# Splitting the weights of two mixers and the first FFN panels one layer ahead, into a pair of parts in DRAM

## The chip, the cores and the metric

The kernel runs on one core of one Trainium2 chip. It is one program that goes once through eight layers. The metric is the device time of one execution in microseconds (us); what counts is the median of several executions. The profile and the trace belong to one further execution, recorded by the hardware profiler.

## The reference

One sequence of 512 tokens with 1024 channels, in float32, passes through four layers of a first block (mixers a, b, c, a) and four of a second (a mixer and an FFN, twice). The change touches the weights of the second block:

```python
def sandwich(x, g_pre, g_post, fn):
    return x + rmsnorm(fn(rmsnorm(x, g_pre)), g_post)

def swiglu(h, w_gate, w_up, w_down):
    return (jax.nn.silu(h @ w_gate) * (h @ w_up)) @ w_down

def even_mixer(t, layer_idx, w_in, lq1, lk1, lq2, lk2, subln, dw_w, dw_b, ln_g, ln_b, w_out, cos, sin):
    proj = t @ w_in
    y_a = diff_attention(proj[..., :3 * DIFF_WIDTH], layer_idx, lq1, lk1, lq2, lk2, subln, cos, sin)
    y_b = conformer_conv(proj[..., 3 * DIFF_WIDTH:], dw_w, dw_b, ln_g, ln_b)
    return jnp.concatenate([y_a, y_b], axis=-1) @ w_out

def odd_mixer(...):
    proj = t @ w_in
    ...
    y_c = s5_ssm(proj[..., :o1], a_re, a_im, ...)
    y_d = mla_attention(proj[..., o1:o2], proj[..., o2:o3], proj[..., o3:], ...)
    return jnp.concatenate([y_c, y_d], axis=-1) @ w_out
```

`diff_attention` takes the softmax of two score maps per head and subtracts one from the other; `conformer_conv` is a causal depthwise convolution of width 31 over 512 channels with a layer norm; `s5_ssm` is a linear recurrence over time; `mla_attention` is attention with compressed keys and values. Each weight matrix is used once per execution.

## The kernel before

**Stages.** The layers run in the order a0, b, c, a1, m0 (the even mixer), f0 (its FFN), m1 (the odd mixer), f1. In the trace c lies at about 950 to 1255 us, a1 to 1642, m0 to 1950, f0 to 2330, m1 to 2575 and f1 to the end. Activations are held transposed, as eight tiles of 128 channels x 512 tokens.

**Products in three parts.** A float32 product is made on TensorE (PE) from three products of fp32r operands (`mm3`, L287): each factor is split into a high part h, the value rounded to fp32r, and a low part l, the rest; then h·h, h·l and l·h are summed in PSUM. So each weight chunk, usually 128 x 1024 float32 or 512 KB, goes through three steps in `wchunk` (L273): SyncE (SP) issues its load into a tile `wr` (`fetch`, L252 to L255), ScalarE (ACT) copies it rounded into `wh` (L280), and VectorE (DVE) writes `wl` = `wr` - `wh` (L284; in the profile the line is L205, that of the wrapper that records every PE and DVE operation). The pool `pw` holds three buffers each of `wr`, `wh` and `wl`, so a chunk can be fetched and split while PE still works on the ones ahead.

**Who splits.** GpSimd (POOL) takes over the subtraction in two places: in m0, from `project(0)` on, for every third chunk (`share`, L271 to L276), and in `sandwich_end` for the chunks W1 and W2 (L975, L989). It does so in two pieces of 512 columns, whose rows carry the line L284.

**Panels.** `gemm_T` (L328) makes one output panel of 128 channels: a chunk, 24 matmuls of 512 tokens, and then a `tick()`. `gemm_tok` (L363) makes a token-major product from four chunks of the same size, with a tick after each. A tick advances every generator in the list `tasks` by one step (L296); `drain()` (L301) runs them to their end. Attention heads, the convolution and the tables of the recurrence are such tasks. The tasks settle the program order. Outside pinned stretches a scheduler then sets a fixed order for each engine, and every engine works through its own order one instruction after another, each with its waits. So an instruction that waits holds up all that stands behind it on that engine.

**m0.** Eight panels (`m0_wab`) yield the convolution's input. The convolution (`conv`, L1074) then runs as a task: per tile of 128 channels, 23 taps on DVE, as one multiply and 22 multiply-adds into the tile `cv`, and 8 taps on ACT and POOL into `cvg` (L1092). Meanwhile PE makes the projections for heads 0 and 1 (`project(0)`), the values, and `project(1)`. DVE also turns the query and key tiles by their rotary angles (the tiles `t`) and takes the maximum of each row of scores (`Ps`, `mxc`), which the exponential of the softmax needs. The scores lie in PSUM tiles called `a`; the panels' sums in those called `g`.

**m1.** The panels of `m1_win` come first, then keys, values and queries (`m1_wk`, `m1_wv`, `m1_wq`), while the recurrence runs as a task, with its scans and products on DVE (tiles `t`) and tables `E` and `bc` loaded from DRAM. They were stored there by `ssm_tables`, a task in f0 (L1595).

**Ends.** Each mixer of the second block and each FFN ends in `sandwich_end` (L891): the last output panels, the norm, the update of the eight tiles of x, and the first four panels of the layer that follows (W0 to W3 from `srcs`), which are thus split ahead, inside the end of the layer before. PE's and DVE's orders are fixed by hand there.

**c.** `layer_c` (L828) has two halves; each runs, twice, four panels of `c_wx`, four of `c_wz` and four half-size ones of `c_wg`, and then eight of `c_wo`.

Of the kernel before, what the change touches and what calls it, by code (L numbers as in the profile page):

```python
# [4 lines left out]
P = 128  # L5
# [174 lines left out]
def build(nc, tc, A, out, stages=("a0", "b", "c", "a1", "m0", "f0", "m1", "f1")):  # L180
# [40 lines left out]
    with ctx:  # L221
# [48 lines left out]

        share = [0, 0]  # L271

        def wchunk(src, n, eng=None):  # L273
            if eng is None:
                share[1] += 1
                eng = G if share[0] and share[1] % share[0] == 0 else V  # L276
            wr = early.pop(0) if early else fetch(src, n)
            wh = tl(pw, (P, 1024), "wh", F32R)
            wl = tl(pw, (P, 1024), "wl", F32R)
            S.activation(wh[:, :n], wr[:, :n], AF.Copy)  # L280
            step = n if eng is V else 512
            for o in range(0, n, step):
                e = slice(o, o + step)
                eng.tensor_tensor(wl[:, e], wr[:, e], f32(wh[:, e]), op=SUB)  # L284
            return wh, wl
# [542 lines left out]
        def layer_c(nxt):  # L828
            with ExitStack() as c:
# [7 lines left out]
                for t in pads:  # L837
                    V.memset(t[:, 0:16], 0.0)
                npad = [0]

# [4 lines left out]
                for half in range(2):  # L845
                    Y = []
                    for g in (2 * half, 2 * half + 1):
                        wd = 2 << g
                        M = []
                        for i in range(4):  # L850
                            ps = first.pop(0) if first else gemm_T(A["c_wx"][g * 4 + i], X)
                            xc = pad()
                            V.tensor_tensor(xc[:, 16:], ps, sb, op=MUL)
                            a, sh = xc, 1
                            while sh < wd:
                                b = pad() if sh * 2 < wd else tl(pp, (P, 16 + NT), "last", bufs=2)
                                (G if sh > 1 else V).tensor_tensor(
                                    b[:, 16:], a[:, 16:], a[:, 16 - sh:16 + NT - sh], op=ADD)
                                a, sh = b, sh * 2
                            df = tmp()  # L860
                            V.scalar_tensor_tensor(df, a[:, 16:], 1.0 / wd, xc[:, 16:], op0=MUL, op1=SUB)
                            fx = tl(psm, (P, 16), "fx")
                            V.tensor_tensor(fx, a[:, 16:32], ic[:, g * 16:g * 16 + 16], op=MUL)
                            V.tensor_tensor(df[:, :16], fx, xc[:, 16:32], op=SUB)
                            M.append(split(pp5, "m", df))
                        Z = []
                        for i in range(4):
                            pz = gemm_T(A["c_wz"][g * 4 + i], X)
                            z = tl(pp, (P, NT), "z", bufs=5)
                            V.tensor_tensor(z, pz, sb, op=MUL)  # L870
                            S.activation(z, z, AF.Silu)
                            Z.append(z)
                        for i in range(4):
                            ps = gemm_T(A["c_wg"][g, i], M)
                            V.scalar_tensor_tensor(Z[i], ps, csc[:, g * 4 + i:g * 4 + i + 1], Z[i],
                                                   op0=MUL, op1=MUL)
                            Y.append(split(py, "y", Z[i]))
                    for m in range(KD):
                        ps = gemm_T(A["c_wo"][half, m], Y)
                        V.tensor_tensor(xs[m], xs[m], ps, op=ADD)  # L880
                        if half:
                            finish_x(m)()

        def ffn_first(l):
            return [A[f"f{l}_w{n}"][i] for i in range(2) for n in "gu"] if f"f{l}" in stages else None

        def m1_first():
            return [A["m1_win"][i] for i in (2, 0, 1, 3)] if "m1" in stages else None


        def sandwich_end(W, Y, O, fresh, grow, srcs, pre=None, k0=0):  # L891
# [82 lines left out]
            if srcs:  # L974
                W1 = wchunk(srcs[1], D, G)  # L975
            begin(c, two)
# [3 lines left out]
            if srcs is None:  # L980
# [7 lines left out]
                return  # L988
            W2 = wchunk(srcs[2], D, G)  # L989
            X = state["X"]  # L990
# [54 lines left out]
        def layer_m0(nxt):  # L1045
            with ExitStack() as c:
                pm = newpool(c, "pm")
                pa = newpool(c, "pm0a", 8)
                X = state["X"]
                first, sc, sb = opening([A["m0_wab"][i] for i in range(3)], X)  # L1050
                new_norm(nxt)
# [75 lines left out]
                for i in range(4):  # L1127
                    pu = first.pop(0) if first else gemm_T(A["m0_wab"][2 * i], X)
                    pb = first.pop(0) if first else gemm_T(A["m0_wab"][2 * i + 1], X)
                    b = tmp()  # L1130
# [13 lines left out]
                def project(a):  # L1144

                    pss = gemm_tok([A["m0_wqk"][a, i] for i in range(4)], X, NT, 2)
                    q = tl(pm, (P, 4, 8, 64), "qk")
# [26 lines left out]
                def attend(h, T):  # L1174
# [53 lines left out]
                tasks.append(attend(3, T[1]))  # L1228
                share[0] = 0
                while any(Y[k] is None for k in range(4)):  # L1230
                    tick()
                sandwich_end(A["m0_wo"], Y, [tl(pa, (P, NT), "qkT") for _ in range(KD)], True, 8, ffn_first(0), k0=4)


# [132 lines left out]
        def layer_m1(nxt):  # L1367
            with ExitStack() as c:
# [91 lines left out]
                def glu():  # L1460
# [3 lines left out]
                    yield  # L1464
                    wh, wl = wchunk(A["s_wg"], 512)
                    for m in range(2):
# [26 lines left out]
                for i in range(2):  # L1493
                    ps = gemm_T(A["m1_win"][4 + i], X)
                    ss.add(ps, i)
                    CQ.append(split(py, "y", ps, qg[:, i:i + 1]))
# [4 lines left out]

                wh, wl = wchunk(A["m1_wk"], 768)
                KN = []
                for h in range(6):
# [6 lines left out]
                    if h % 2:  # L1511
                        tick()
                wh, wl = wchunk(A["m1_wv"], 768)
                vt = tl(pm, (P, 4, 768), "vt")
# [10 lines left out]
                for a in range(3):  # L1525
                    wh, wl = wchunk(A["m1_wq"][a], 1024)
                    for b in range(4):
# [51 lines left out]
                O = [t[:, a] for t in [tl(pm, (P, 2, NT), "E", bufs=3) for _ in range(3)] for a in range(2)]  # L1579
                sandwich_end(A["m1_wo"], Y, O + [tl(pm, (P, NT), f"u{i}") for i in range(2)], True, 10, ffn_first(1))  # L1580


        def layer_f(l, nxt):
            with ExitStack() as c:
# [30 lines left out]

        pdr0 = newpool(ctx, "pdr0", space=bass.MemoryType.DRAM)
        mag = tl(pc, (P, 8), "mag")
# [41 lines left out]
```

## Time and profile before

| what | value |
| --- | --- |
| median of 3 executions | 2931.03 us |
| lowest, highest | 2930.87, 2932.01 us |
| the profiled execution, its own time | 2936.18 us |
| span of the profiled execution | 2933.7 us |
| mean granted TensorE clock over the span | 0.976 of full speed |
| PE busy | 2820.6 us, 96% |
| DVE busy | 1642.2 us, 56% |
| ACT busy | 1051.9 us, 36% |
| POOL busy | 347.3 us, 12% |
| moved by DMA | 270.08 MB, 92 GB/s over the span |

The profiled execution's own time is that of the device; the span is what the profiler saw from its first to its last instruction, and 2.5 us lie around it. Busy time counts an engine's instructions and not its waits. PE is the engine that is busy nearly all the time; its clock can be lowered by the chip, and the granted clock says by how much in a stretch.

### The profile page before, as it was taken

Reading aid. Unit: us, or ns where it says so; the run is one execution under the profiler, and the core shown is the slowest. Engines: PE = TensorE matmul, PEld = TensorE weight load, DVE = VectorE, ACT = ScalarE, POOL = GpSimd, SP = SyncE. Lnnn points to the kernel's source line nnn. Section 1 sums busy time; section 2 is a strip of 40 time slices with the busy share of each in tenths; the row PEclk is TensorE's granted clock in tenths of the full one; section 3 lists DMA queues with packets and bytes.
Section 4 is the critical chain, followed back from the end, with each engine's and each line's share of the span. In section 5 each row is a group of like instructions: output and inputs, shape, how many; then the busy total and the mean of one; then the engine's idle time right before and its main releaser. Section 6 shows DMA issues by size and latency. Waiting matters only on the chain. (4 is left out here: it accounts for less than half of the span.)

```text
span 2933.7 us, 34524 instructions
## 1 busy us (share of the span) xinstructions
PE 2820.6 (96%) x13488; PEld 2331.9 (79%) x13488; DVE 1642.2 (56%) x3023; ACT 1051.9 (36%) x1679; POOL 347.3 (12%) x272
## 2 busy tenths in 40 slices
PE   8999999999999999999999987889999979999998
PEld 7888888888888888888888865678888845888886
DVE  4454654545556554544445697896443696543434
ACT  4322344444444322333223445442222435432222
POOL 2000000000000111210010252120000341300001
PEclk9999999999999999999999997889999999999999
DMA  4222332222223232322222211123332320132222
GB/s 161 94 86 94 129 111 87 87 80 94 72 94 95 94 101 89 120 93 94 93 94 92 90 63 44 48 96 136 111 105 92 113 90 22 58 101 100 94 99 67
DMA packets 87667, 270.08 MB, mean 92 GB/s; under 512 B 11728, under 2 KB 18640, under 8 KB 87504
## 3 DMA queue, kind: packets, MB, share of 16 engines
q1 hardware_dynamic: 87504, 267.88, 27.6%
q8 instruction: 105, 1.72, 0.2%
q14 instruction: 58, 0.48, 0.1%
HBM read 255.26 MB, written 12.58 MB: 91 GB/s over the span
## 5 line engine op out<-in xcount | busy, mean ns | idle before, releaser
L280 ACT ACTIVATE wh<-wr 128x1024 fp32r<-128x1024 f32 (+2 forms) x464 | 479.9, 1035 | 1329.8 <-PE g L205 1015.7
L205 DVE TENSOR_TENSOR wl<-wr,wh 128x1024 fp32r<-128x1024 f32 (+2 forms) x454 | 566.3, 1248 | 341.3 <-ACT wh L280 338.7
L205 PE MATMUL g<-xl,wh 128*128 128x512 f32 (+1 forms) x1720 | 661.6, 385 | 17.2 <-DVE xl L205 17.0
L205 PE MATMUL g<-xh,wh 128*128 128x512 f32 (+1 forms) x1720 | 663.7, 386 | 0.7 <-ACT wh L280 0.7
L205 PE MATMUL g<-xh,wl 128*128 128x512 f32 (+1 forms) x1720 | 658.1, 383 | 0.8 <-DVE wl L205 0.8
L205 PE MATMUL g<-wh,xh 128*128 128x512 f32 (+1 forms) x992 | 383.1, 386 | 16.9 <-ACT wh L280 8.9
L205 PE MATMUL g<-yh,wh 128*128 128x512 f32 (+1 forms) x1046 | 394.9, 378 | 1.4 <-DVE qr L205 1.4
L205 PE MATMUL g<-yh,wl 128*128 128x512 f32 (+1 forms) x1046 | 391.4, 374 | 3.1 <-DVE wl L205 3.1
L205 PEld LDWEIGHTS g<-xl,wh 128*128 128x128 f32 x1720 | 327.1, 190 | 83.0 <-DVE xl L205 22.9
L205 PE MATMUL g<-yl,wh 128*128 128x512 f32 (+1 forms) x1046 | 391.2, 374 | 0.0
L205 PE MATMUL g<-wl,xh 128*128 128x512 f32 (+1 forms) x992 | 377.8, 381 | 0.5 <-DVE wl L205 0.5
L205 PEld LDWEIGHTS g<-xh,wl 128*128 128x128 f32 x1720 | 327.3, 190 | 63.2 <-DVE wl L205 1.4
L205 PE MATMUL g<-wh,xl 128*128 128x512 f32 (+1 forms) x992 | 376.6, 380 | 0.0
L205 PEld LDWEIGHTS g<-xh,wh 128*128 128x128 f32 x1720 | 327.5, 190 | 61.2 <-ACT wh L280 1.2
L424 POOL TENSOR_TENSOR acc<-acc,t 128x256 f32<-128x256 f32 (+1 forms) x111 | 129.8, 1170 | 1654.5 <-issue 1406.4
L205 PEld LDWEIGHTS g<-wh,xh 128*128 128x128 f32 x992 | 188.5, 190 | 50.4 <-ACT wh L280 8.9
L205 PEld LDWEIGHTS g<-yh,wh 128*128 128x128 f32 x1046 | 198.4, 190 | 37.9 <-DVE qr L205 1.8
L205 PEld LDWEIGHTS g<-yh,wl 128*128 128x128 f32 x1046 | 198.1, 189 | 38.1 <-DVE wl L205 4.2
L205 PEld LDWEIGHTS g<-yl,wh 128*128 128x128 f32 x1046 | 198.3, 190 | 35.4 <-issue 1.2
L205 DVE TENSOR_TENSOR t<-g,sb 128x512 f32<-128x512 f32 x112 | 77.2, 690 | 251.4 <-PE g L205 251.4
L205 PEld LDWEIGHTS g<-wh,xl 128*128 128x128 f32 x992 | 188.4, 190 | 34.7 <-issue 0.2
L205 PEld LDWEIGHTS g<-wl,xh 128*128 128x128 f32 x992 | 188.6, 190 | 33.9 <-DVE wl L205 1.6
(315 smaller groups left out, 2728.5 us busy)
## 6 DMA issues: line engine op xcount, KB each, us to landing
wr<-in_f_wg_dram SPq DMA_DIRECT2D x44, 512.0 KB, 3.5
wr<-in_f_wu_dram SPq DMA_DIRECT2D x44, 512.0 KB, 3.5
wr<-in_a_wv_dram SPq DMA_DIRECT2D x32, 512.0 KB, 3.5
wr<-in_a_wu_dram SPq DMA_DIRECT2D x32, 512.0 KB, 3.4
wr<-in_a_wz_dram SPq DMA_DIRECT2D x32, 512.0 KB, 3.4
wr<-in_a_wo_dram SPq DMA_DIRECT2D x32, 512.0 KB, 3.5
wr<-in_b_wc_dram SPq DMA_DIRECT2D x32, 512.0 KB, 3.5
wr<-in_f_wd_dram SPq DMA_DIRECT2D x32, 512.0 KB, 3.5
```

The source lines that it names most:

```text
L205: r = f(*a, **k)
L280: S.activation(wh[:, :n], wr[:, :n], AF.Copy)
L424: G.tensor_tensor(self.acc[:, t], self.acc[:, t], sq[:, t], op=ADD)
```

## The change

A class `Pre` names a chunk together with two DRAM tiles for its parts, h and l. A task `presplit` makes them: per step SP loads a chunk into the tile `pr`, ACT writes `ph`, DVE writes `pl`, and SP stores both parts to DRAM. `pr` has one buffer, `ph` and `pl` have two each. A step ends right after its load was issued, and its split comes with the next tick. `wchunk` of a `Pre` then loads the parts straight into `wh` and `wl` by two DMAs and splits nothing. The sharing with POOL is gone, for these chunks and for W1 and W2.

The task runs twice: in c, for the 28 chunks of m0 and the first four panels of f0; and in f0 from its third pair of panels on, beside `ssm_tables`, for the 20 chunks of m1 and the first four panels of f1. Layer c drains it before its last eight panels.

```diff
-
-        def wchunk(src, n, eng=None):
-            if eng is None:
-                share[1] += 1
-                eng = G if share[0] and share[1] % share[0] == 0 else V
-            wr = early.pop(0) if early else fetch(src, n)
+        pdr0 = newpool(ctx, "pdr0", space=bass.MemoryType.DRAM)
+
+        class Pre:
+
+
+            def __init__(self, src, n):
+                uid[0] += 1
+                self.src, self.n = src, n
+                self.h, self.l = (tl(pdr0, (P, n), f"pre{a}{uid[0]}") for a in "hl")
+
+        def presplit(pool, todo):
+            made = []
+
+            def store():
+                w, wh, wl = made.pop(0)
+                nc.sync.dma_start(w.h, f32(wh))
+                nc.sync.dma_start(w.l, f32(wl))
+            for w in todo:
+                n = w.n
+                wr = tl(pool, (P, 1024), "pr")[:, :n]
+                wh, wl = (tl(pool, (P, 1024), "p" + a, F32R, bufs=2)[:, :n] for a in "hl")
+                nc.sync.dma_start(wr, w.src)
+                if made:
+                    store()
+                yield
+                S.activation(wh, wr, AF.Copy)
+                V.tensor_tensor(wl, wr, f32(wh), op=SUB)
+                made.append((w, wh, wl))
+            store()
+
+        def wchunk(src, n):
             wh = tl(pw, (P, 1024), "wh", F32R)
             wl = tl(pw, (P, 1024), "wl", F32R)
+            if isinstance(src, Pre):
+                nc.sync.dma_start(f32(wh[:, :n]), src.h)
+                nc.sync.dma_start(f32(wl[:, :n]), src.l)
+                return wh, wl
+            wr = early.pop(0) if early else fetch(src, n)
             S.activation(wh[:, :n], wr[:, :n], AF.Copy)
-            step = n if eng is V else 512
-            for o in range(0, n, step):
-                e = slice(o, o + step)
-                eng.tensor_tensor(wl[:, e], wr[:, e], f32(wh[:, e]), op=SUB)
+            V.tensor_tensor(wl[:, :n], wr[:, :n], f32(wh[:, :n]), op=SUB)
             return wh, wl
 
         def mm3(ps, ah, al, bh, bl, start, stop):
...
                     V.memset(t[:, 0:16], 0.0)
+                if "m0" in stages:
+                    tasks.append(presplit(newpool(c, "pre"), m0_weights() + (ffn_first(0) or [])))
                 npad = [0]
 
...
                             V.scalar_tensor_tensor(Z[i], ps, csc[:, g * 4 + i:g * 4 + i + 1], Z[i],
                                                    op0=MUL, op1=MUL)
                             Y.append(split(py, "y", Z[i]))
+                    if half:
+                        drain()
                     for m in range(KD):
                         ps = gemm_T(A["c_wo"][half, m], Y)
                         V.tensor_tensor(xs[m], xs[m], ps, op=ADD)
                         if half:
                             finish_x(m)()
 
+        PRE = {}
+
+        def pre(name, *ix):
+            k = (name,) + ix
+            if k not in PRE:
+                a = A[name]
+                for i in ix:
+                    a = a[i]
+                PRE[k] = Pre(a, a.shape[-1])
+            return PRE[k]
+
         def ffn_first(l):
-            return [A[f"f{l}_w{n}"][i] for i in range(2) for n in "gu"] if f"f{l}" in stages else None
+            return [pre(f"f{l}_w{n}", i) for i in range(2) for n in "gu"] if f"f{l}" in stages else None
 
         def m1_first():
-            return [A["m1_win"][i] for i in (2, 0, 1, 3)] if "m1" in stages else None
+            return [pre("m1_win", i) for i in (2, 0, 1, 3)] if "m1" in stages else None
+
+        def m0_weights():
+            return ([pre("m0_wab", i) for i in range(8)] + [pre("m0_wqk", a, i) for a in range(2) for i in range(4)]
+                    + [pre("m0_wv", i) for i in range(4)] + [pre("m0_wo", m) for m in range(KD)])
+
+        def m1_weights():
+            return (m1_first() + [pre("m1_win", i) for i in (4, 5)] + [pre("m1_wk"), pre("m1_wv")]
+                    + [pre("m1_wq", a) for a in range(3)] + [pre("s_wg")] + [pre("m1_wo", m) for m in range(KD)])
 
 
         def sandwich_end(W, Y, O, fresh, grow, srcs, pre=None, k0=0):
...
             if srcs:
-                W1 = wchunk(srcs[1], D, G)
+                W1 = wchunk(srcs[1], D)
...
-            W2 = wchunk(srcs[2], D, G)
+            W2 = wchunk(srcs[2], D)
...
-                share[:] = [3, 0]
                 q = project(0)
                 T = [flip_qk(q, 0), flip_qk(q, 1)]
-                pss = gemm_tok([A["m0_wv"][i] for i in range(4)], X, NT, 2)
...
                         if l == 0 and i == 2 and "m1" in stages:
+                            tasks.append(presplit(newpool(c, "pre"), m1_weights() + (ffn_first(1) or [])))
                             tasks.append(ssm_tables(ptab))
                         pg = first.pop(0) if first else gemm_T(A[f"f{l}_wg"][i], X)
                         pu = first.pop(0) if first else gemm_T(A[f"f{l}_wu"][i], X)
```

The other uses of m0's and m1's weights are changed in the same way, from `A["m0_wo"][m]` to `pre("m0_wo", m)` and so on. `pdr0` moves from the end of `build` to this place.

In the orders below, an operation's output stands before the arrow and its inputs behind it.

DVE in m0, before, at the first row maximum of the attention. `cv` are taps of the convolution, `wl` low parts of weights, `ISA Ps` the maximum.

```order
L205 TENSOR_TENSOR wl_13345<-wr_13342,wh_13344 128x1024
L205 SCALAR_TENSOR_TENSOR cv_2314_12738<-up_2313_12735,m_dw_12571,cv_2314_12738 128x512
L205 SCALAR_TENSOR_TENSOR cv_2327_12822<-up_2326_12819,m_dw_12571,cv_2327_12822 128x512
L205 SCALAR_TENSOR_TENSOR cv_2314_12738<-up_2313_12735,m_dw_12571,cv_2314_12738 128x512
L205 SCALAR_TENSOR_TENSOR cv_2327_12822<-up_2326_12819,m_dw_12571,cv_2327_12822 128x512
L205 ISA Ps_13266,mxc_13267<-a_13264,cmask_12592 128x128
L205 ISA mxc_13267 128x1
L205 ISA Ps_13272,mxc_13273<-a_13270,cmask_12592 128x128
L205 ISA mxc_13273 128x1
```

DVE at the same place, after.

```order
L205 SCALAR_TENSOR_TENSOR cv_2500_13050<-up_2499_13047,m_dw_12889,cv_2500_13050 128x512
L205 SCALAR_TENSOR_TENSOR cv_2511_13130<-up_2510_13127,m_dw_12889,cv_2511_13130 128x512
L205 TENSOR_TENSOR cv_2500_13050<-cv_2500_13050,cvg_13424 128x512
L205 SCALAR_TENSOR_TENSOR cv_2511_13130<-up_2510_13127,m_dw_12889,cv_2511_13130 128x512 x14
L205 ISA Ps_13553,mxc_13554<-a_13551,cmask_12910 128x128
L205 ISA mxc_13554 128x1
L205 ISA Ps_13559,mxc_13560<-a_13557,cmask_12910 128x128
L205 ISA mxc_13560 128x1
L205 RECIPROCAL d_2576_13550<-d_2576_13550 128x2
```

The first maximum now stands behind all 88 multiply-adds of the convolution, where 78 stood ahead of it before, and no `wl` lies among them.

SP in c, before, at the half's output panels: one fetch per panel.

```order
L254 DMA wr_8571<-in_c_wg_dram 128x512
L254 DMA wr_8595<-in_c_wo_dram 128x1024
L254 DMA wr_8627<-in_c_wo_dram 128x1024
L254 DMA wr_8659<-in_c_wo_dram 128x1024
L254 DMA wr_8691<-in_c_wo_dram 128x1024
```

SP at the same panels, after: `pr` is the load of the chunk that is split ahead, `preh` and `prel` are the stores of its parts.

```order
L254 DMA wr_8908<-in_c_wo_dram 128x1024
L286 DMA preh_1497_7917<-ph_8784 128x1024
L292 DMA pr_8815<-in_m_wo_dram 128x1024
L287 DMA prel_1498_7918<-pl_8785 128x1024
L254 DMA wr_8948<-in_c_wo_dram 128x1024
L286 DMA preh_1500_7919<-ph_8816 128x1024
L292 DMA pr_8859<-in_m_wo_dram 128x1024
L287 DMA prel_1501_7920<-pl_8817 128x1024
L254 DMA wr_8988<-in_c_wo_dram 128x1024
```

Each fetch of a panel now stands behind the load of `pr` and both stores; the load of `pr` itself cannot start before DVE has written the `pl` before it, since there is one buffer.

ACT at these panels, after.

```order
L296 ACTIVATE ph_8816<-pr_8815 128x1024
L309 ACTIVATE wh_8946<-wr_8948 128x1024
L296 ACTIVATE ph_8860<-pr_8859 128x1024
L309 ACTIVATE wh_8986<-wr_8988 128x1024
L296 ACTIVATE ph_8900<-pr_8899 128x1024
L309 ACTIVATE wh_9026<-wr_9028 128x1024
```

A `ph` now stands ahead of each `wh`, one for one; before, `wh` alone stood for the weights here. The task's last 13 chunks go in this way, one beside each full panel; counted back further, its last 20 go beside 19 full panels and four half ones.

## Rows read from the trace of the kernel before

**Rows 1.** The page's part 1: busy us (share of the span), number of instructions.

```profile
PE 2820.6 (96%) x13488; PEld 2331.9 (79%) x13488; DVE 1642.2 (56%) x3023; ACT 1051.9 (36%) x1679; POOL 347.3 (12%) x272
```

**Rows 2.** Windows (c, m0, m1): length; PE, PEld, DVE, ACT, POOL; clock; DMA; GB/s.

```profile
1100.00:1150.00 50.00, 50.00 (x223) 41.39 (x222) 21.82 (x32) 10.83 (x12) 8.99 (x6) 1.00 0.27 89
...
1700.00:1750.00 50.00, 44.23 (x188) 36.22 (x187) 49.65 (x62) 22.70 (x36) 29.60 (x18) 0.91 0.16 53
1750.00:1800.00 50.00, 37.61 (x166) 27.80 (x164) 42.80 (x85) 21.14 (x48) 12.73 (x9) 0.86 0.18 64
1800.00:1850.00 50.00, 42.56 (x156) 27.65 (x152) 32.26 (x97) 31.53 (x82) 12.50 (x10) 0.66 0.03 11
...
1900.00:1950.00 50.00, 40.44 (x253) 38.32 (x253) 47.90 (x152) 20.92 (x46) 20.45 (x22) 0.80 0.21 75
...
2400.00:2450.00 50.00, 35.35 (x123) 18.93 (x121) 43.08 (x74) 18.29 (x39) 21.98 (x17) 0.80 0.12 40
```

**Rows 3.** Windows of 105.5 and 79 us: m0's convolution; m1's recurrence.

```profile
1665.00:1770.50 105.50, 80.77 (x346) 65.39 (x344) 105.08 (x126) 41.42 (x61) 50.49 (x30) 0.90 0.20 67
2338.00:2417.00 79.00, 60.50 (x248) 42.27 (x246) 74.58 (x96) 25.51 (x40) 35.12 (x26) 0.94 0.32 108
```

**Rows 4.** Waits of PE, m0, by window: total us, times, longest.

```profile
PE g L205 <- DVE t L205: 8.0, 1, 8.0
...
PE a L205 <- DVE mxc L205: 10.8, 1, 10.8
```

**Rows 5.** Timeline of DVE ahead of m0's first row maximum: start, duration, operation.

```profile
1743.41 14.91 DVE L205 SCALAR_TENSOR_TENSOR cv<-up,m_dw,cv 128x512 f32<-128x512 f32 x13
1758.25 1.21 DVE L205 TENSOR_TENSOR wl<-wr,wh 128x1024 fp32r<-128x1024 f32 x1
...
1770.49 0.28 DVE L205 CUSTOM_DVE_ANT_0 Ps<-a,cmask 128x128 f32<-128x128 f32 x1
```

**Rows 6.** Groups of DVE, then of POOL, 1665 to 1770 us: busy, mean ns.

```profile
L205 DVE SCALAR_TENSOR_TENSOR cv<-up,m_dw,cv 128x512 f32<-128x512 f32 x78 | 76.4, 1030 | 0.0
L205 DVE TENSOR_TENSOR wl<-wr,wh 128x1024 fp32r<-128x1024 f32 x10 | 16.0, 1603 | 0.4 <-ACT wh L280 0.4
...
L1092 POOL TENSOR_TENSOR cvg<-cvg,t 128x512 f32<-128x512 f32 x21 | 36.0, 1716 | 39.1 <-ACT t L1091 25.8 <-ACT cvg L1085 12.4
L284 POOL TENSOR_TENSOR wl<-wr,wh 128x512 fp32r<-128x512 f32 x8 | 12.9, 1628 | 9.8 <-ACT wh L280 9.8
```

**Rows 7.** The tiles `cv` and `wl` on DVE, same stretch: min/median/max ns.

```profile
L205 DVE SCALAR_TENSOR_TENSOR cv<-up,m_dw,cv x78: 733/740/1895, 1666.5 to 1769.8; 128x512 f32<-128x512 f32 x78
...
L205 DVE TENSOR_TENSOR wl<-wr,wh x10: 1206/1212/2314, 1670.8 to 1766.7; 128x1024 fp32r<-128x1024 f32 x10
```

**Rows 8.** Groups of DVE in m1, 2338 to 2417 us: low parts.

```profile
L205 DVE TENSOR_TENSOR wl<-wr,wh 128x1024 fp32r<-128x1024 f32 x4 | 6.0, 1507 | 0.0
L205 DVE TENSOR_TENSOR wl<-wr,wh 128x768 fp32r<-128x768 f32 x2 | 1.9, 953 | 1.3 <-PE a L205 1.3
```

**Rows 9.** Waits of PE in m1, 2340 to 2500 us.

```profile
PE a L205 <- DVE t L205: 9.9, 1, 9.9
```

**Rows 10.** Timeline of ACT in c, two panels in a row: start, duration.

```profile
1085.59 1.06 ACT L280 ACTIVATE wh<-wr 128x1024 fp32r<-128x1024 f32 x1 [3.84 <-issue]
1091.03 1.06 ACT L280 ACTIVATE wh<-wr 128x1024 fp32r<-128x1024 f32 x1 [4.38 <-PE g L205]
```

**Rows 11.** DMA issues, KB, median us to landing: c; then 2320 to 2350 us.

```profile
wr<-in_c_wx_dram SPq DMA_DIRECT2D x16, 512.0 KB, 3.4
...
E<-srot SPq DMA_DIRECT2D x3, 512.0 KB, 7.6
```

**Rows 12.** Windows in that crowded stretch, 10 us and 2 us.

```profile
2330.00:2340.00 10.00, 10.00 (x63) 8.94 (x63) 5.36 (x13) 3.91 (x6) 1.02 (x1) 1.00 1.00 358
2338.00:2340.00 2.00, 2.00 (x18) 1.95 (x17) 1.27 (x3) 1.22 (x2) 0.00 (x0) 1.00 1.05 427
```

More of the change, by code (lines that the diff above doesn't have):

```diff
@@ L1049, in layer_m0 @@
                 X = state["X"]
-                first, sc, sb = opening([A["m0_wab"][i] for i in range(3)], X)
+                first, sc, sb = opening([pre("m0_wab", i) for i in range(3)], X)
                 new_norm(nxt)
@@ L1127, in layer_m0 @@
                 for i in range(4):
-                    pu = first.pop(0) if first else gemm_T(A["m0_wab"][2 * i], X)
-                    pb = first.pop(0) if first else gemm_T(A["m0_wab"][2 * i + 1], X)
+                    pu = first.pop(0) if first else gemm_T(pre("m0_wab", 2 * i), X)
+                    pb = first.pop(0) if first else gemm_T(pre("m0_wab", 2 * i + 1), X)
                     b = tmp()
@@ L1144, in project @@
                 def project(a):
-                    pss = gemm_tok([A["m0_wqk"][a, i] for i in range(4)], X, NT, 2)
+                    pss = gemm_tok([pre("m0_wqk", a, i) for i in range(4)], X, NT, 2)
                     q = tl(pm, (P, 4, 8, 64), "qk")
@@ L1215, in attend @@
                     Y[4 + h] = split(py, "y", ps, sub)
-                share[:] = [3, 0]
                 q = project(0)
                 T = [flip_qk(q, 0), flip_qk(q, 1)]
-                pss = gemm_tok([A["m0_wv"][i] for i in range(4)], X, NT, 2)
+                pss = gemm_tok([pre("m0_wv", i) for i in range(4)], X, NT, 2)
                 vt = tl(pm, (P, 4, NT), "vt")
@@ L1228, in layer_m0 @@
                 tasks.append(attend(3, T[1]))
-                share[0] = 0
                 while any(Y[k] is None for k in range(4)):
                     tick()
-                sandwich_end(A["m0_wo"], Y, [tl(pa, (P, NT), "qkT") for _ in range(KD)], True, 8, ffn_first(0), k0=4)
+                sandwich_end([pre("m0_wo", m) for m in range(KD)], Y, [tl(pa, (P, NT), "qkT") for _ in range(KD)], True, 8, ffn_first(0), k0=4)
         def ssm_tables(p):
@@ L1464, in glu @@
                     yield
-                    wh, wl = wchunk(A["s_wg"], 512)
+                    wh, wl = wchunk(pre("s_wg"), 512)
                     for m in range(2):
@@ L1493, in layer_m1 @@
                 for i in range(2):
-                    ps = gemm_T(A["m1_win"][4 + i], X)
+                    ps = gemm_T(pre("m1_win", 4 + i), X)
                     ss.add(ps, i)
@@ L1512, in layer_m1 @@
                         tick()
-                wh, wl = wchunk(A["m1_wv"], 768)
+                wh, wl = wchunk(pre("m1_wv"), 768)
                 vt = tl(pm, (P, 4, 768), "vt")
@@ L1525, in layer_m1 @@
                 for a in range(3):
-                    wh, wl = wchunk(A["m1_wq"][a], 1024)
+                    wh, wl = wchunk(pre("m1_wq", a), 1024)
                     for b in range(4):
@@ L1579, in layer_m1 @@
                 O = [t[:, a] for t in [tl(pm, (P, 2, NT), "E", bufs=3) for _ in range(3)] for a in range(2)]
-                sandwich_end(A["m1_wo"], Y, O + [tl(pm, (P, NT), f"u{i}") for i in range(2)], True, 10, ffn_first(1))
+                sandwich_end([pre("m1_wo", m) for m in range(KD)], Y, O + [tl(pm, (P, NT), f"u{i}") for i in range(2)], True, 10, ffn_first(1))
         def layer_f(l, nxt):
```

4 lines of the change are left out of this document (1 added, 3 removed).

## The prediction

> **What bounds the kernel now.** The page's first part gives the frame: PE is busy for 2820.6 us, 96% of the span, and DVE for 56% [rows 1]. A mean says nothing of a stage, so the windows come next. In layer c PE is busy for 50 of 50 us at full clock while DVE works 21.8 us and the DMA engines are used to 0.27 [rows 2]: c is bound by PE and has room elsewhere. In m0 it is the other way: DVE is busy for 49.65 of 50 us, PE idles, and the clock falls to 0.86 and then to 0.66, so part of the time is spent at the lower of PE's two levels [rows 2]. Over the 105.5 us of m0 in which the convolution runs, DVE works 105.08 us and PE 80.77 [rows 3]. There DVE sets the pace. The waits say so too: PE waits 8.0 us for DVE's `t`, and 10.8 us for the first row maximum `mxc` [rows 4]. The timeline shows why that maximum is late: taps of the convolution and low parts of weights stand ahead of it without a gap, and it runs at 1770.49 [rows 5]. In m1 the recurrence does the same for 79 us, with DVE at 74.6 and PE at 60.5 [rows 3], and PE waits 9.9 us for `t` [rows 9].
>
> So the change takes work from DVE and POOL where DVE is the bound, and puts it where PE is, together with 1 MB of stores for each 0.5 MB chunk.
>
> **m0, the gain.** Ten low parts leave DVE ahead of the first maximum. They took 16.0 us [rows 6], where the shortest takes 1.21 [rows 7], so 12.1 us are their own work and 3.9 are lost. The 78 taps took 76.4 us [rows 6] against a least of 0.74 each [rows 7], 57.7 in all: 18.7 us lost. Together 22.6 us of slowing stand beside 50.5 us of POOL [rows 3], which I take as its cause, as the long taps run while POOL adds. POOL's own low parts, 12.9 us of it [rows 6], go away: 22.6 x 12.9 / 50.5 = 5.8 us back. Against that, the order puts ten more taps and one more sum ahead of the first maximum: 11 x 0.74 = 8.1 us. So it comes 12.1 + 5.8 - 8.1 = 9.8 us earlier. These 8.1 us are missing behind it, where project(1)'s rotary work and the softmax follow; DVE is partly idle there (42.8 of 50 us [rows 2]), so I credit 3 of them. m0: **-12.8 us**. Its bounds: 0 if the order eats it all, and -24.7, all of PE's idle time in the stretch [rows 3].
>
> What was hidden and is uncovered: a chunk now needs two loads in sequence after PE has freed its buffers. One lands after 3.4 us [rows 11], the second 0.5 MB / 427 GB/s [rows 12] = 1.2 us later: 4.6 us, against two panels of 5.44 us (from the pitch of `wh`, 1085.59 to 1091.03 [rows 10]) that three buffers leave. That is hidden in m0's and m1's panels.
>
> **m1, the gain.** Six low parts take 6.0 + 1.9 = 7.9 us from a DVE that is busy 94% of that stretch [rows 3, 8]; one small one more is neglected. Its start is crowded by loads of tables already, where a 512 KB load takes 7.6 us [rows 11], and the new loads double the weights' bytes: +1. m1: **-6.9 us**, between -7.9 and, with the loads late by what the crowded load is above the common one (4.2 us), -3.7.
>
> **Three ends of layers.** W1 was ready 1.06 [rows 10] + 2 x 1.63 [rows 6] = 4.3 us after its buffer was free, now after 4.6: +0.3. W3 was ready after 1.06 + 1.21 = 2.3 us, with half a panel pair, 2.7 us of PE work, ahead of it; now it takes 4.6, so PE stands for 1.9. That makes +2.2 per end. Back come W0's 1.2 us on DVE and the slowing by POOL's four pieces, 6.5 us x 22.6 / 50.5 = 2.9, where DVE is at 47.9 of 50 [rows 2]; I credit under half, 1.9. Three ends: 3 x 0.3, say **+1**; bounds 3 x (2.2 - 4.1) = -6 and 3 x 2.2 = +7.
>
> **c, the cost.** 32 chunks are split ahead. ACT and DVE have the time. But `pr` has one buffer, and so one step is a chain: load, `ph`, `pl`, next load. With a load that finds the queue empty it lasts 3.4 [rows 11] + 1.06 [rows 10] + 1.21 [rows 7] = 5.7 us. But the store of `ph` was issued one `pl` before each load; with all of its 0.5 MB ahead the load lands 1.2 us later, and the step lasts 6.9. I take 6.5, nearer to the upper, as the hand-overs between engines aren't in the sum. A full panel is 5.44 us. Since `ph` and `wh` alternate on ACT, and the panel's fetch stands behind the task's DMAs on SP, the panels of c follow this chain wherever it is slower than PE. The last 20 steps lie beside 19 full and four half panels, 21 x 5.44 = 114 us, and the buffers give two panels, 11 us, of reserve. The cost is 20 T - 125 us: 0 at 5.7, **+5** at 6.5, +13 at 6.9. The nearest row for a queue that is never empty is the load of 7.6 us [rows 11], T = 9.9 and +73; but that was at a DMA share of 1.00 [rows 12], and 2.1 MB in 6.5 us are 323 GB/s.
>
> The Trainium skill has a rule against the change here: "DMA: Bandwidth & Descriptors", section "Where 436 GB/s comes from", says that the HBM side, some 358 GB/s for a core, binds transfers between HBM and SBUF. The trace shows 358 GB/s over 10 us and 427 over the best 2 us of them [rows 12], so it isn't a limit here; were it one, the 323 GB/s would fill it to 90% instead of 76%, and the first rival would weigh more.
>
> **f0, the cost.** 24 steps beside some 28 panels, 152 us, and 11 of reserve: 24 x 6.5 = 156 fits. **+1** for the work put beside the tables; 0 to +3 at T = 6.9.
>
> **Sum.** -12.8 - 6.9 + 1 + 5 + 1 = -12.7 us. The profiled execution took 2936.2 us, of which 2933.7 are its span, and lies 5.2 above the median of the runs. So 2936.2 - 12.7 - 5.2 = 2918.3: I forecast **2918 us**. Taps that lose more or less, the ends and T between 5.7 and 6.9 make 2908 to 2929 of this case.
>
> **Rivals.**
>
> 1. *The chain in c and f0 becomes the bound* (slower). If other DMAs, the panel's fetch among them, keep a load for 0.8 us more than I take, T is 7.3: c costs 20 x 7.3 - 125 = 21 and f0 24 x 7.3 - 163 = 12 us. Then -12.8 - 6.9 + 1 + 33 = +14.3, or 2945. It decides at 44 T - 288 = 18.7, T = 7.0. For it speaks the single buffer, and that four DMAs share the queue in each step; against it that c used the DMA engines to 0.27 [rows 2].
> 2. *The first maximum comes no earlier* (gain hidden). The order puts more taps ahead of it. If POOL's sums slow the taps as before and the third `cvg`, which now stands ahead too, comes late, m0 gains nothing: -6.9 + 1 + 5 + 1 = 0, or 2931. For it speaks that POOL's sums are paced by ACT; against it that 12.9 us of POOL are gone.
> 3. *The clock holds.* Between 1800 and 1850 PE works 42.6 us at a clock of 0.66 [rows 2], after the long waits of m0. If shorter waits leave it at 2.4 GHz, these take 42.6 x 0.34 = 14.5 us less: 2904. Against it speaks that the attention itself leaves PE little work at a time.
>
> That the splits come out of m0 and m1 isn't in doubt: the order shows no `wl` there.
>
> **How the numbers follow.** Forecast 0.50, rival 1 0.20, rival 2 0.18, rival 3 0.12. About 0.2%, 6 us, is what a measurement of this kernel can tell from no change: faster is below 2925.2, slower above 2936.9. Of the forecast's 0.50, 0.43 lie below 2925, the rest within: faster 0.43 + 0.12 = 0.55; same 0.07 + 0.17 = 0.24; slower 0.20 and 0.01 of rival 2. The range of 2902 to 2945 leaves out half of rival 1 and some of rival 3. The likeliest case's own range, 2908 to 2929, stands above, as most of the chance lies on one side.
>
> **What would show it.** Step by step: m0's first row maximum at some 95 us after the convolution's first tap instead of 105; no wait over 2 us for it; taps nearer to 0.74 us. In m1 the wait of 9.9 us for `t` mostly gone. In the ends a new wait of about 2 us for a load into `wh` or `wl`. In c, steps of `ph` 6.5 us apart or less, and PE's windows still full but for some 5 us; if PE idles there for 20 us with waits for ACT or a load, rival 1 is right. If the clock between 1800 and 1850 rises above 0.9, rival 3. Wrong altogether it would be if DMA into `wh` and `wl` became PE's main wait in m0.

## The result, and the profile after

| | before | after |
| --- | --- | --- |
| median | 2930.95 us (2927.76 to 2932.01, 4 executions) | 2954.92 us (2952.76 to 2964.61, 4 executions) |
| ratio | | 1.009, 95% interval 1.0066 to 1.0114 |
| profiled execution, span | 2933.7 us | 2954.3 us |

The change makes the kernel 24 us slower. The forecast was 2918 us, in a range of 2902 to 2945. The sign was that of the first rival, and the size is beyond it.

The page of the changed kernel, part 1 and the sums of part 3 (as [rows 1]):

```profile
PE 2826.7 (96%) x13488; PEld 2327.1 (79%) x13488; DVE 1635.8 (55%) x3033; ACT 1052.0 (36%) x1679; POOL 306.6 (10%) x252
...
HBM read 312.94 MB, written 70.25 MB: 130 GB/s over the span
```

The sums hide the result: PE's busy time grows by 6 us only. What tells is the start of the same instruction in both traces. From one landmark to the next, the difference is what a stage gained or lost. These are the changes in us against the profiled execution of before, for the changed kernel and the seven experiments below (`u` is the recurrence's input; the last row compares medians of runs, e4's of one run):

| from, to | after | e1 gain alone | e2 two pr | e4 no store | e5 in place | e3 spread | e6 one pr | e7 W3 |
| --- | --- | --- | --- | --- | --- | --- | --- | --- |
| c: end of b to the row sums of a1 | +37.5 | +3.4 | +28.4 | +9.8 | +12.8 | -0.1 | -0.2 | -0.1 |
| m0: first tap to its last update of x | -19.3 | -19.0 | -19.3 | -18.4 | -17.9 | -18.3 | -18.0 | -19.1 |
| f0, to its first scaled output | +9.0 | -1.5 | +9.2 | +6.9 | +9.7 | -0.1 | +1.0 | -2.4 |
| end of f0, to m1's first `u` | +2.6 | +2.1 | +2.3 | +1.3 | +0.7 | +1.1 | +2.5 | -0.4 |
| m1: first `u` to its last update of x | -9.4 | -4.7 | -9.9 | -6.2 | -9.7 | -7.9 | -8.9 | -7.2 |
| whole, to the last scaled output | +21.0 | -20.3 | +12.2 | -6.7 | -4.8 | -24.5 | -23.7 | -28.7 |
| medians, less before's beside them | +24.0 | -13.1 | +19.0 | +1.4 | +5.5 | -14.2 | -14.1 | -19.7 |

The parts not listed (the start, a1, f1) stay within 2 us. So against this one execution of before, m0 and m1 gain 28.7 us together, and c, f0 and its end lose 49.1. But its own time, 2936.18 us, lies 5.2 us above the median that it belongs to and 7.6 to 8.8 above before's medians beside the experiments, at a granted clock of 0.976 where 17 of those 20 runs show 0.979 to 0.982. That is most of why the whole stands 3 to 10 us below the medians in each column. In c, and in f0 up to 2300 us, the trace of before shows a clock of 1.00, so it is mainly the gains of m0 and m1 that come out too large. With the medians, the change's +24.0 less 49.1 leaves a gain of 25.1, and e3's -14.2 less its costs of 0.9 leaves 15.1; the forecast was 19.7. That m0 and m1 gain more than forecast is thus not shown.

**c.** Windows of the changed kernel, columns as in [rows 2]:

```profile
950.00:1000.00 50.00, 44.43 (x194) 36.71 (x193) 29.59 (x38) 20.77 (x25) 8.68 (x6) 0.93 0.85 295
...
1050.00:1100.00 50.00, 45.57 (x191) 36.64 (x190) 32.35 (x46) 21.60 (x28) 4.81 (x3) 0.95 0.86 297
1100.00:1150.00 50.00, 47.39 (x199) 37.20 (x199) 23.14 (x25) 15.37 (x15) 0.00 (x0) 0.99 0.86 294
1150.00:1200.00 50.00, 40.84 (x156) 30.32 (x155) 30.48 (x41) 17.08 (x20) 10.95 (x8) 0.93 0.75 257
```

Where PE was busy for 50 of 50 us and the DMA engines at 0.27 [rows 2], they now stand at 0.75 to 0.86, and PE is idle for up to 9 us in 50. The rhythm is on ACT; here are two steps at c's output panels, its timeline (start, duration, operation, and in brackets the idle time ahead and what ended it):

```profile
1127.73 1.06 ACT L296 ACTIVATE ph<-pr 128x1024 fp32r<-128x1024 f32 x1 [3.36 <-DMA pr<-in_m_wo_dram]
1130.22 1.06 ACT L309 ACTIVATE wh<-wr 128x1024 fp32r<-128x1024 f32 x1 [1.43 <-DMA wr<-in_c_wo_dram]
1134.60 1.06 ACT L296 ACTIVATE ph<-pr 128x1024 fp32r<-128x1024 f32 x1 [3.31 <-DMA pr<-in_m_wo_dram]
```

A step takes 6.9 us (1127.73 to 1134.60), and a panel's `wh` comes once in a step, no sooner: ACT waits for `pr`, splits it, then waits 1.43 us for the panel's own fetch, which was issued behind three other DMAs. In before, `wh` came every 5.44 us [rows 10]. SP's timeline of one step shows that order:

```profile
1142.65 0.33 SPq L286 DMA_DIRECT2D preh<-ph  x1
1143.91 0.33 SPq L292 DMA_DIRECT2D pr<-in_m_wo_dram  x1
1144.29 0.45 SPq L287 DMA_DIRECT2D prel<-pl  x1
1144.79 0.42 SPq L254 DMA_DIRECT2D wr<-in_c_wx_dram  x1
1149.77 0.33 SPq L286 DMA_DIRECT2D preh<-ph  x1
1151.03 0.33 SPq L292 DMA_DIRECT2D pr<-in_m_wo_dram  x1
```

The load waits for `pl`, 1.26 us after the store of `ph`, and the next step's load goes out 7.1 us later. Its landing, over c's last part (1100 to 1195 us):

```profile
DMA to landing us min/median/max: 4.4/4.6/5.5
```

Against 3.4 us alone [rows 11]. 4.6 + 1.06 + 1.22 = 6.9 us, the step.

By the starts of the same matmuls in both traces, PE loses the 37.5 us in three places: 10 by 1000 us, 9 between 1085 and 1106 us, at the half-size panels of `c_wg`, and 18 between 1134 and 1193 us. At the first of them DVE's timeline shows how a waiting step holds up c's own work:

```profile
991.34 1.23 DVE L205 TENSOR_TENSOR pl<-pr,ph 128x1024 fp32r<-128x1024 f32 x1 [4.49 <-ACT ph L296]
```

Behind this `pl` stands, in DVE's order, the first step to the diagonal of c's scales, and PE waits 5.6 us for that diagonal. At the half-size panels a step of the task, as long as anywhere, stands beside 2.7 us of PE work instead of 5.44.

**m0.** The stretch that answers to [rows 3], from the convolution's first tap to the first row maximum, and DVE's timeline there, as in [rows 5]:

```profile
1702.50:1800.00 97.50, 82.34 (x345) 66.20 (x343) 96.72 (x125) 26.41 (x46) 40.24 (x25) 0.92 0.43 151
```

```profile
1795.35 4.69 DVE L205 SCALAR_TENSOR_TENSOR cv<-up,m_dw,cv 128x512 f32<-128x512 f32 x6
1799.96 0.29 DVE L205 CUSTOM_DVE_ANT_0 Ps<-a,cmask 128x128 f32<-128x128 f32 x1
```

The stretch is 96.7 us long, from 1703.3 to 1800.0, where it was 104.6. The longest wait for `mxc` is halved from 10.8 us [rows 4]; waits of PE between 1690 and 1962 us:

```profile
PE a L205 <- DVE mxc L205: 6.4, 3, 4.9
PE g L205 <- DMA wh<-preh: 5.7, 2, 4.4
```

The 4.4 us are one load into `wh` at m0's end, for which PE waits at 1919 us; the forecast had 1.9, for another chunk (W3). SP's timeline and its own wait show why this load was late:

```profile
1913.95 0.32 SPq L1411 DMA_DIRECT2D srot<-E  x1
1914.37 0.38 SPq L305 DMA_DIRECT2D wh<-preh  x1
```

```profile
SPq L1411 <- DVE eu L205: 9.5, 1, 9.5
```

In SP's order it stands behind `srot<-E`, the store of a table for m1's recurrence, and SP waited 9.5 us for DVE to finish that table. PE waits 4.3 to 5.1 us at this place in the change and in each of the seven experiments, e7 too; the forecast hadn't counted it, and no run moved the store.

Behind the maximum, PE's windows are better off than the 0.66 of [rows 2]:

```profile
1840.00:1850.00 10.00, 8.43 (x36) 4.63 (x37) 8.67 (x27) 9.29 (x24) 0.78 (x1) 1.00 0.00 0
1850.00:1860.00 10.00, 6.98 (x43) 5.19 (x43) 7.66 (x29) 7.28 (x20) 4.89 (x5) 0.79 0.00 1
1860.00:1870.00 10.00, 8.65 (x42) 5.89 (x41) 8.59 (x20) 6.59 (x13) 0.00 (x0) 0.87 0.00 1
```

In the trace of before two windows lie wholly at PE's lower level, 1.2 GHz, here:

```profile
1820.00:1830.00 10.00, 9.31 (x33) 6.56 (x32) 6.11 (x17) 5.89 (x16) 2.95 (x3) 0.50 0.00 0
1830.00:1840.00 10.00, 6.48 (x27) 5.25 (x26) 4.38 (x17) 3.02 (x9) 2.84 (x3) 0.50 0.00 0
```

As that execution's clock was below that of most others, how much of this difference the change made isn't shown.

**m1.** Its long wait for the recurrence is as long as in [rows 9]; it only comes earlier. Waits of PE, 2369 to 2530 us:

```profile
PE a L205 <- DVE t L205: 10.6, 2, 9.9
```

**f0.** One wait of PE between 2036 and 2062 us, ACT's timeline at it, and windows of 5 us:

```profile
PE g L205 <- ACT yh L418: 2.3, 1, 2.3
```

```profile
2048.93 0.63 ACT L296 ACTIVATE ph<-pr 128x512 fp32r<-128x512 f32 x1 [1.93 <-DMA pr<-in_s_wg_dram]
2049.46 0.61 ACT L418 ACTIVATE yh<-t 128x512 fp32r<-128x512 f32 x1
2051.74 1.06 ACT L309 ACTIVATE wh<-wr 128x1024 fp32r<-128x1024 f32 x1 [1.66 <-PE g L205]
```

```profile
2045.00:2050.00 5.00, 2.84 (x13) 2.03 (x11) 3.06 (x4) 2.45 (x4) 0.00 (x0) 1.00 0.92 320
2050.00:2055.00 5.00, 4.76 (x13) 3.56 (x14) 3.21 (x4) 1.13 (x2) 0.00 (x0) 0.66 0.95 304
```

`yh`, the FFN's own activation, stands in ACT's order behind a `ph` that waits for its load. PE waits 2.3 us for it, and in the next 5 us the clock is at 0.66; together this costs 4.4 of f0's 9.0 us. Another 3.5 go between 2140 and 2153 us, where PE waits for `wh` and `wl`.

### The profile page after: what moved, and what is told of

It reads as the page before. It is cut to its first block, busy times and chain, and to the rows that moved or that the text cites. A ratio compares the mean times of both kernels' runs of the same rounds, so it can differ in the third digit from the quotient of the medians.

```text
span 2954.3 us, 34865 instructions
## 1 busy us (share of the span) xinstructions
PE 2826.7 (96%) x13488; PEld 2327.1 (79%) x13488; DVE 1635.8 (55%) x3033; ACT 1052.0 (36%) x1679; POOL 306.6 (10%) x252
## 5 line engine op out<-in xcount | busy, mean ns | idle before, releaser
L309 ACT ACTIVATE wh<-wr 128x1024 fp32r<-128x1024 f32 (+2 forms) x408 | 420.8, 1033 | 1037.0 <-PE g L205 789.2
L205 DVE TENSOR_TENSOR wl<-wr,wh 128x1024 fp32r<-128x1024 f32 (+2 forms) x408 | 508.7, 1247 | 307.0 <-ACT wh L309 304.3
L205 PE MATMUL g<-xl,wh 128*128 128x512 f32 (+1 forms) x1720 | 661.3, 384 | 13.5 <-DVE xl L205 13.4
L205 PEld LDWEIGHTS g<-xh,wl 128*128 128x128 f32 x1720 | 327.0, 190 | 77.0 <-DVE wl L205 10.8
```

The lines of the kernel that those rows point to most:

```text
L205: r = f(*a, **k)
```

## The experiments

**e1: the gain without the work ahead.** All parts are loaded from one DRAM pair per width, and only its one chunk is split:

```diff
+                if n not in ONE:
+                    ONE[n] = self
...
+                self.h, self.l = ONE[n].h, ONE[n].l
-            for w in todo:
+            for w in [w for w in todo if ONE[w.n] is w]:
```

> Only the first chunk of each width is split ahead; m0, m1 and the FFNs' first panels load all their parts from that one DRAM pair, so the weights of these layers are not the right ones here. The loads into wh and wl and the missing splits stay as in the change, and the work in c and f0 is gone. Theory 1 (all the loss lies where the splits were moved to): layer c is as before within 2 us, f0 within 4; m0 stays about 19 us and m1 about 7 us shorter than before, the whole at 2900 to 2908 us. Theory 2 (the loads into wh and wl cost something in m0, m1 and the ends that the gain hides): it stays above 2915 us, with PE waits for these loads.

Measured: 2914.23 us against 2927.35, ratio 0.9948 (0.9929 to 0.9966). Nearly all of the loss in c and f0 is gone, and m0's gain of 19 us against the trace of before is there: theory 1 holds for where the loss lies. c still loses 3.4 us: 1.9 where b ends and its single chunk is split, and 1.6 at 1220 to 1230 us, where the clock is at 0.83. The time is 6 us over the range that was named, since that range was built on gains against an execution of before that is 8.8 us above the median here. Theory 2 isn't out: the time is within 1 us of its bound, and PE waits for loads into `wh` and `wl` in this run, 4.5 us of it in the wait behind `srot<-E`:

```profile
PE g L205 <- DMA wh<-preh: 10.4, 6, 4.5
PE g L205 <- DMA wl<-prel: 3.2, 5, 0.8
```

**e2: two load buffers.** For room, `ph` gave up one:

```diff
-                wr = tl(pool, (P, 1024), "pr")[:, :n]
-                wh, wl = (tl(pool, (P, 1024), "p" + a, F32R, bufs=2)[:, :n] for a in "hl")
+                wr = tl(pool, (P, 1024), "pr", bufs=2)[:, :n]
+                wh, wl = (tl(pool, (P, 1024), "p" + a, F32R, bufs=b)[:, :n] for a, b in (("h", 1), ("l", 2)))
```

> The load tile pr has two buffers, and ph one in exchange for the room; all else is the change. Theory A (the chain of load, ph, pl, next load through the one buffer sets the pace of c): the next load now runs during ph and pl, a step falls from 7.0 to 7.7 us to about 5.5, c loses under 12 us instead of 37, f0 about 3 instead of 10, the whole is near 2923 us. Theory B (2.1 MB of traffic per panel through the queue sets the pace): the step stays at 7 us, and the time within 5 us of the changed kernel's 2955.

Measured: 2946.35 us against 2927.35, ratio 1.0066 (1.0041 to 1.0092); c loses 28.4 us instead of 37.5. Neither theory's number came, and the timeline of ACT says why the run can't decide:

```profile
1118.92 1.06 ACT L296 ACTIVATE ph<-pr 128x1024 fp32r<-128x1024 f32 x1 [1.58 <-DMA preh<-ph]
1121.42 1.06 ACT L309 ACTIVATE wh<-wr 128x1024 fp32r<-128x1024 f32 x1 [1.44 <-DMA wr<-in_c_wo_dram]
1124.00 1.06 ACT L296 ACTIVATE ph<-pr 128x1024 fp32r<-128x1024 f32 x1 [1.51 <-DMA preh<-ph]
```

`ph` no longer waits for its load but for the store of the `ph` before to land. One chain was traded for another.

**e4: no stores.** All loads and splits, but a store only for the first chunk of a width:

```diff
+                if ONE[w.n] is w:
+                    nc.sync.dma_start(w.h, f32(wh))
+                    nc.sync.dma_start(w.l, f32(wl))
```

> Every chunk is loaded ahead and split in c and f0 as in the change, but only the first of each width is stored, and all parts are loaded from that pair later, so most weights of the later layers are not the right ones here. The traffic in c falls from 2.1 to 1.05 MB per panel. Theory A (chain through one pr buffer, with a load that lands late because the stores share the queue): the load lands after 3.4 to 3.8 us, the step takes 5.9 to 6.3, c loses at most 8 us. Theory B (traffic alone): c loses nothing. Theory D (the added ph and pl delay ACT and DVE work that PE waits for): c still loses 20 us or more, with waits of PE for wl or mh.

Measured: 2928.71 us, one execution; c loses 9.8 us. Loads of `pr` from 1090 to 1200 us, and ACT's timeline:

```profile
DMA to landing us min/median/max: 3.3/3.4/4.5
```

```profile
1115.88 1.06 ACT L302 ACTIVATE ph<-pr 128x1024 fp32r<-128x1024 f32 x1 [3.46 <-DMA pr<-in_m_wo_dram]
1116.85 1.04 ACT L315 ACTIVATE wh<-wr 128x1024 fp32r<-128x1024 f32 x1
1121.71 1.06 ACT L302 ACTIVATE ph<-pr 128x1024 fp32r<-128x1024 f32 x1 [3.83 <-DMA pr<-in_m_wo_dram]
```

The load lands after 3.4 us, the step takes 5.8, and it still leads: ACT waits for `pr`. So the chain is there without the stores, as theory A says, and the stores lengthen it by the later landing: 1.2 us. But a step of 5.8 beside panels of 5.44 us cost PE nothing here; what e4 loses, it loses for the most part ahead of them, at the half-size panels:

```profile
1075.00:1095.00 20.00, 15.02 (x60) 10.78 (x60) 15.10 (x20) 10.71 (x14) 0.00 (x0) 1.00 0.67 211
1095.00:1150.00 55.00, 55.00 (x244) 45.52 (x244) 30.79 (x35) 20.13 (x20) 3.00 (x2) 1.00 0.59 184
```

Theory D, work alone, is out for most of the loss; theory B's nothing did not come either.

**e5: no chain, all the traffic.** `pl` overwrites the loaded chunk, so three such tiles and two `ph` fit:

```diff
+                pr = tl(pool, (P, 1024), "pr", F32R, bufs=3)[:, :n]
+                wr = f32(pr)
+                wh, wl = tl(pool, (P, 1024), "ph", F32R, bufs=2)[:, :n], pr
```

> As the change, at its full rate in c, but pl is written over the loaded chunk, and there are three such tiles and two ph. So neither the next load nor the next ph waits for a store or for pl of the step before, which the version with two pr and one ph still did (its ph waited for the store of the last ph). Theory A (a chain through buffers sets the step): steps near 5.5 us, c loses under 12 us, the whole near 2917 to 2925 us. Theory B (2.1 MB per panel through one queue): steps stay at 6.3 us or more with the DMA engines near full, c loses 20 us or more, the whole at 2938 us or above.

Measured: 2934.11 us against 2928.63, ratio 1.0022 (1.0009 to 1.0034). The time lies between the two theories' numbers. In the trace c loses 12.8 us, so 24.7 of the 37.5 are gone with the chain; but that execution, 2930.36 us, is among the fastest of ten (2928.58 to 2943.48). By the medians 18.5 us are gone, half of c's loss if all of it lies there. What is left looks like traffic, as theory B has it: the DMA engines are full ahead of the output panels, at 383 GB/s over 30 us, and PE idles when the buffers have run out.

```profile
1080.00:1110.00 30.00, 30.00 (x134) 24.70 (x133) 20.25 (x22) 13.85 (x15) 0.00 (x0) 1.00 1.02 383
1100.00:1150.00 50.00, 44.06 (x185) 35.34 (x184) 26.66 (x32) 16.01 (x17) 5.93 (x4) 0.97 0.88 316
```

PE idles for 6 us in the second window, and a load of `pr` takes 7.3 us (median of eight, `in_m_wo`). f0 loses 9.7 us, as much as in the change, but in other places: PE waits 7.1 us for `wl`, in five pieces.

**e3: spread out.** 16 chunks in c at one in three panels, 16 in a1 as halves, f0 at one in two:

```diff
+                tc.keep_in_program_order(nc.sync.dma_start(wr, w.src))
...
+                steps += 1
+                while ticks < steps * pace:
+                    ticks += 1
+                    yield
...
+                    tasks.append(presplit(newpool(c, "pre"), todo[:16], 3.0))
```

The first line keeps a load behind the fetch that was written ahead of it. Without it, the scheduler's order is said to have put the steps as early as the buffers let it, whatever the ticks said; no run here shows that.

> The same splits are spread out: 16 of the 32 chunks in c at one per three panels, 16 in a1 as half chunks at one half per 1.75 panels, and m1's 24 in f0 at one per two panels; each load ahead is kept behind the fetch of the panel it is written beside, and pr has two buffers, ph one. Theories A and B both say that a step of 7 us beside 10.9 to 16 us of panels costs nothing: c, a1 and f0 within 3 us of before each, the whole at 2903 to 2912 us. Theory D says that the same work of ACT and DVE still delays panels, by about as much per chunk: over 2930 us.

Measured: 2913.14 us against 2927.35, ratio 0.9948 (0.9932 to 0.9965): faster than before by 14 us. c's windows are full again, at 0.45 to 0.59 of the DMA engines:

```profile
950.00:1000.00 50.00, 50.00 (x230) 41.66 (x229) 30.24 (x46) 18.70 (x25) 9.72 (x6) 1.00 0.45 155
1100.00:1150.00 50.00, 50.00 (x223) 41.40 (x222) 24.56 (x33) 12.72 (x13) 8.99 (x6) 1.00 0.50 174
1150.00:1200.00 50.00, 50.00 (x222) 41.43 (x221) 31.09 (x45) 20.18 (x26) 10.60 (x8) 1.00 0.59 205
```

The same splits, half of c's moved to a1, cost nothing at this pace, in f0 too (-0.1). Theory D is out. The median is 1 us above the range named, which, like e1's, was built on gains against the one execution of before.

**e6: spread, with the change's own buffers.**

```diff
-                wr = tl(pool, (P, wide), "pr", bufs=2)[:, :n]
+                wr = tl(pool, (P, wide), "pr")[:, :n]
...
+                wh, wl = (tl(pool, (P, wide), "p" + a, F32R, bufs=2)[:, :n] for a in "hl")
```

> The spread version with the change's own buffers: one pr, two ph, two pl. It differs from the version that was spread with two pr in the buffers alone. If pace is what counts, the chain of 7 us is hidden beside 9.5 us or more of panels in each step, and the time is the same within 3 us, c and a1 as before within 2 us. If the buffers did it, c loses again, 8 us or more.

Measured: 2914.53 us against 2928.63, ratio 0.9945 (0.9929 to 0.9962), c at -0.2 us. One buffer is enough where a step has more than its 7 us of time. The pace and the fixed place of the load were changed together; which share each has wasn't tried, as no slow pace came about without the other.

**e7: the fourth panel split at its place**, from a tile fetched early, for the three ends:

```diff
-            return [pre("m1_win", i) for i in (2, 0, 1, 3)] if "m1" in stages else None
+            return [pre("m1_win", i) for i in (2, 0, 1)] + [A["m1_win"][3]] if "m1" in stages else None
```

> The spread version with two pr, but the fourth panel of f0, m1 and f1 is fetched early and split at its place, as in the kernel before. Theory: at each of the three ends PE stood for 1.7 and 0.8 us for the two loads into a buffer that had just been freed; split from a tile fetched early it is ready sooner by about 2.4 us, so each end gains 1.5 to 2.5 us, together 4 to 7 us: 2906 to 2910 us. Rival: the split's work on DVE lies in the stretch where DVE is the bound there, and the ends gain nothing or lose.

Measured: 2908.91 us against 2928.63, ratio 0.9925 (0.9909 to 0.9941), the fastest of all and 20 us below before. It stands 4.2 us below e3 in the profiles. m0 with its end gains 0.8 of it and f0's end 1.5; m1 with its end loses 0.7, and f1 gains 0.3. The remainder, 2.3 us, stands in the table's row of f0 but belongs to m0's end: e3's wait for W3, 1.7 us at 1931, comes behind the last update of x at 1924.5, where that row starts. At m0's end (1890 to 1935 us), waits of PE for loads fell from these in e3

```profile
PE g L205 <- DMA wh<-preh: 3.3, 2, 1.7
PE g L205 <- DMA wl<-prel: 1.1, 2, 0.8
```

to these in e7:

```profile
PE g L205 <- DMA wh<-preh: 1.6, 1, 1.6
PE g L205 <- DMA wl<-prel: 0.8, 1, 0.8
```

So one of the two waits is gone there, that for W3. The 1.7 and 0.8 us of the expectation are the other one, for W1 (its load goes out at 1895.5 us and PE takes it up at 1900.5); it stays. Against the rival, DVE's added work cost less than it saved, at two of the three ends.

## Why the prediction was wrong, point by point

**c, the step that failed.** The chain was named, with its place and its decisive point (T = 7.0), but its term was sized +5 and measured +37.5. Three things in it fell. First, T: I took 6.5 between 5.7 and 6.9, and the trace shows 6.9 to 7.9 at the output panels and 7.1 to 8.2 at the panels behind them. The unloaded end was right (5.8 in e4), and so was the mechanism that lengthens it; but 6.9 was the lowest value there and no upper end. Second, only the last 20 steps were counted, with 11 us of reserve as if nothing had been spent ahead of them. All 31 steps, from the `ph` at 939.8 to the last at 1186.7, took 246.9 us, 8.0 us each, and 10 us were lost in the first panels already, 5.6 of them in one wait for the diagonal of c's scales. Third, the sum set the steps against the panels' total, with four half panels as two full ones. But a step has to fit beside its own panel: 9 us went at the half-size ones, and e4, where 20 T - 125 at T = 5.8 gives no loss, lost 6.5 us there. The last 20 steps took 147.9 us, 7.4 each; in the formula that gives 23, and the first panels' 10 come on top. The remaining 5 aren't told apart. At the `c_wx` panels the `mh` of c's own pooling stands between `ph` and `wh` on ACT, and the panels' `wh` come up to 8.8 us apart there.

**f0** was +1 and measured +9.0. The sum asked whether steps of 6.5 us fit beside the panels. They do on average; but half of the cost is a `yh` behind a waiting `ph`, once 2.3 us, and then a slower clock, which no sum of steps shows. e5 and e4 keep 9.7 and 6.9 of it without the chain or the stores, e3 nothing.

**Rival 1** was the right one, at a chance of 0.20. By its formula its price, 33 us, was too low by 13.5 us for the reasons above. The chance was too small as well: my own T and its decisive point lay 0.5 us apart, and the sum behind T left out the hand-overs between the engines, by its own words.

**m0** was -12.8 and measured -19.3 against the trace of before. The first maximum came 7.9 us earlier, which puts rival 2 out, where 9.8 were worked out: the taps took 82.3 us for 88 and not the 79 that the sum amounts to:

```profile
L205 DVE SCALAR_TENSOR_TENSOR cv<-up,m_dw,cv 128x512 f32<-128x512 f32 x88 | 82.3, 982 | 0.7
```

From there to the last maximum 3.1 more came, as credited. What the sum did not have is 6.7 us between the last maximum and the convolution's last `yl`, its low part: POOL's last sum `cvg` is ready 10 us earlier after the first tap, and the granted clock there is 0.66 to 1.00, where the trace of before has 0.50 to 0.75. That is the place of rival 3, but its sign, a clock above 0.9, didn't come (0.83 over the same matmuls), and how much of the 6.7 us lies in that one execution of before isn't shown.

**m1** was -6.9 and measured -9.4, with -4.7 to -9.9 in the other versions. The term was right in size, its sign of proof wrong: the wait of 9.9 us for `t` didn't shrink. The recurrence ends 6 us sooner after its start, and PE's work ahead of the wait does as well.

**The ends** were +1 for three; f0's alone cost 2.6 us in the table. The wait for W3 was of the size named, 1.7 us at m0's end in e3, and e7 took it away there. W1, put at +0.3, makes PE wait 1.7 + 0.8 us there in e3, and that stays in e7.

**The rule of the Trainium skill** on 358 GB/s ("DMA: Bandwidth & Descriptors", "Where 436 GB/s comes from") was set aside for the 427 of [rows 12]. With loads and stores mixed, the changed c moved 257 to 297 GB/s in the windows shown, at a DMA share of 0.75 to 0.86. In e5 c moved 383 GB/s over 30 us at a share of 1.02, with PE busy all the time. So 358 isn't a limit here with stores either, and the rule is no reason for the loss; but a chain at 295 GB/s already had the engines at 0.85, so the 76% that I took from 2 us of loads was too low a use of the queue.

## What to carry to other kernels

Work that is put beside a stage bound by TensorE needs room in each step of its own chain, not in the sum of engine time: load, split and buffer release with the landing time of a loaded queue, against the panel beside it, the shortest panel too. Where every engine works in a fixed order, a background step that waits holds up the stage's own work behind it, so give it a pace well below what fits and fix its place behind the stage's own loads (e3 and e6 did both at once). And when a rival's decisive point lies inside the uncertainty of your own number, it is no rival but half of the forecast.

## What the hardware showed that I had not expected

- A wait of PE of 2.3 us in an FFN that kept it busy otherwise was followed by a granted clock of 0.66 over 5 us, so the stretch cost about twice the wait. The same wait of 2.4 us in e4 was followed by 0.54 over 5 us; five waits of up to 1.5 us in e5's f0 left the clock at 1.00.
- A load lands later with stores in the queue: a 512 KB load landed after 3.4 us without them, after 4.6 at 294 GB/s, and after 7.3 where the step had no chain and the windows moved 316 to 383 GB/s.
- The slowing of DVE beside POOL held. Of the 88 taps, the 63 that ran while POOL did nothing took 0.74 us on average, the 25 beside one of its operations 1.58; before it was 51 at 0.74 and 27 at 1.58.
